# The first part of a down projection as 2x2 blocks with seven products, its sums made in the second block of the up projection

## The chip, the cores and the metric

The kernel runs on one core of one Trainium2 chip. The metric is device time in microseconds of one execution of the program; a profiled execution also gives the span from its first to its last instruction. TensorE (PE in the profile) multiplies, VectorE (DVE) and ScalarE (ACT) do the elementwise work, GpSimd (POOL) and SyncE (SP) issue DMAs here, as ACT does too.

## The reference

One layer of a streaming-encoder block, on x of 2048 tokens by 1024 channels in float32. The change touches only the last two lines' matrix products:

```python
h = rmsnorm(x, norm_mix_pre)
u_pool, u_glu, g_a, g_b = split(h @ w_in)
merged = sigmoid(g_a) * pool_mixer(u_pool, ...) + sigmoid(g_b) * conformer_conv(u_glu, ...)
x = x + rmsnorm(merged @ w_o, norm_mix_post)
h = rmsnorm(x, norm_mlp_pre)
f = square(relu(h @ w_up)) @ w_down        # (2048,1024)@(1024,4096), then (2048,4096)@(4096,1024)
return x + rmsnorm(f, norm_mlp_post)
```

## The kernel before

Activations lie transposed: channels on the 128 partitions, tokens along the free axis. A tile is 128x1024 float32 (512 KB): two chunks of 128 channels by a half block of 512 tokens (a "cell"), or an operand of weights. The 2048 tokens are two blocks b of 1024, each with two halves t.

**A product.** [...] `product` (L289) multiplies one weight tile (512 rows by 256 outputs) with two cells into one PSUM tile of 128x1024: two output chunks times four row chunks times three passes, 24 matmuls of 128x128x512, all issued in `matmuls` (L264, L268). Only this instruction form matters below. Every new weight tile costs one cast and one subtraction (`split_w`, L222, cast at L225), every new cell the same.

**Seven products for eight.** All large matrix products are done as 2x2 blocks with Winograd's seven products, numbered 1 to 7: 1 = A11 B11, 2 = A12 B21, and 5, 6, 3, 7, 4 use sums of blocks on one or both sides. `Octet` (L426) runs the seven for one octet of outputs, 512 rows by 512 columns of w_up with 1024 tokens, in three PSUM tiles (`ps_mm` has 3; x takes 1, 6, 7, 4, z takes 2, y takes 5, 3). `ORDER` is (1, 2, 6, 5, 7, 3, 4); the first two octets of a block are interleaved by `START`.

**up.** `mlp_up` (L1400) has eight octets u = 0 to 7 for each block. Output (m, t) of octet u, after ReLU and square, is stored to DRAM as `fd[b, u, (m, t)]`: m is the pair of chunks within the octet's two pairs, t the token half. `sink` also makes and stores the token sums that down needs ("t1", "t2", "t3", "t4"). Octets 0 and 1 of the second block load their weights' low parts and sums ("kept") rather than make them; the others load w_up and split it.

**down.** 4096 rows are four slabs s of 1024 (octets 2s and 2s+1 of up), 1024 outputs are two octets o. Inside each (s, o, b) stand again 2x2 blocks (outputs by pair of chunks m, rows by m, tokens by half t) with seven products i. A job (s, i, b) is two products, one for each o: `down_product` (L1737) accumulates over the four slabs in PSUM, so one i takes 4 slabs x 2 blocks x 2 octets = 16 products, and 7 x 16 = 112 products are all of down. `last_product` (L1751) takes each sum out into the outputs c00, c01, c11, u. i = 1, the block A11 B11 (rows and outputs of the first pairs, first token half), is "the first part": its result `c00[o, b]` is shared by all four outputs. Jobs run by i in `SHARED` (1, 5, 6, 3, 7), then `ALONE` (4, 2).

**Queues and order.** `load` issues on SP's queue, `store` on ACT's, `aside` on POOL's. Each queue and each engine works in the order a scheduler gives at build time; a DMA whose buffer isn't free holds all behind it on its queue. `lanes` hold background generators; `bg()` (L1475), called after every product, advances them one step. `then(f, octet, i)` (L1557) calls f after product i of an octet. `with behind()` (L170) orders instructions after the main line's last eviction. Pools: `p_big` 28 tiles (all taken by the split token sums of a block in up), `p_tr` 9, `p_fo` 5, weights raw `p_wr` 4, high and low parts 3 each.

**Around the change.** One job of down, `FILL`, is computed before up's second block (`filler`, L1957); its result goes to DRAM and is added in later. It is the first job, (0, 1, 0). In up's second block one lane runs `scales()`: `mlp_scale` (L1374) loads x1d, squares it into tiles of `p_fo` and sums it, for the last norm. During up's last octet the cells of down's first three jobs are loaded and split (L1986), so they lie ready when down begins; in the main loop of down the cells are fetched two jobs ahead and each new weight two at a time.

Of the kernel before, what the change touches and what calls it, by code (L numbers as in the profile page):

```python
# [62 lines left out]
def f32(ap):  # L63
    return ap.bitcast(F32)
# [3 lines left out]
def block_kernel(  # L68
# [616 lines left out]
    class Squares:  # L685
# [22 lines left out]
    p_big = pool("pbig", 28)  # L708
    p_tr = pool("ptr", 9)
    early = ExitStack()  # L710
    p_y = pool("py", 1, early)
    p_ss = pool("pss", 1, early)
    p_v = pool("pv", 2, early)
# [297 lines left out]
                load(zd[b, c - 1, 0], y[c - 1])  # L1011
            yield 1

    pw = [p_const.tile([P, CW], F32R, tag=f"pw{i}", name=f"pw{i}") for i in (0, 1)]

    def pool_weight():
        raw = mk(p_wr, "wr")[:, :CW]
# [356 lines left out]
    def mlp_scale(b, buf):  # L1374

        st = None
        for t in (0, 1):
            sq = Squares(buf)
            for c in range(0, CPS, 2):
                x = [mk(*buf) for _ in (0, 1)]  # L1380
                for i in (0, 1):
                    load(x[i], x1d[b, c + i, t])
                yield 1
                sq.add(x[0])
                sq.add(x[1])
            yield 1
            ss = sq.total()
            yield 1
            if st is None:
                st = root_psum()  # L1390
            root_acc(st, ss, inv_d, t * G)
        yield 1
        r = root_dve(st[:, : 2 * G])
        q = p_const.tile([P, 2 * G], F32, tag=f"q{b}", name=f"q{b}")
        mul(q, r, r)
        for t in (0, 1):
            q2[b, t] = q[:, t * G : (t + 1) * G]
        yield

    def mlp_up(b, parts):  # L1400
        def one(u):
            f = {}
            late = (b and u >= 2) or u >= 4

            def sink(m, t, ps, s):
                o = tr()
                if s is not None:
                    mark(add(o, ps, s))
                    ps = o
                mark(nc.scalar.activation(o, ps, AF.Relu))  # L1410
                nc.scalar.activation(o, o, AF.Square)
# [254 lines left out]

    def scales():
# [31 lines left out]
    def token_cells(s, i, b, home=TR, hi_home=BIG):  # L1699

        ready = s >= 2 or (b and s)
        a, m = {
            7: ("t3", None),
            1: ((0, 0), None),
            2: ((1, 0), None),
            6: ("t2", None) if ready else ("t3", (0, 0)),
            4: ("t4", None),
            5: ("t1", None) if ready else ((0, 1), (0, 0)),
            3: ((1, 1), None),
        }[i]  # L1710
        with tc.high_priority(offset=AHEAD):
            cells = []
            for j in (0, 1):
                u = 2 * s + j
                lo = mk(*home, F32R)
                t = f32(lo)
                load(t, fd[b, u, a])
                if m is not None:
                    t2 = mk(*home)
                    load(t2, fd[b, u, m])  # L1720
                    (add if i == 6 else sub)(t2, t, t2)
                    t = t2
# [7 lines left out]
                nc.scalar.copy(hi, t)  # L1730
                sub(lo, t, f32(hi))
                cells.append((hi, lo))
        return cells
# [1 line left out]
    acc = {}  # L1735

    def down_product(s, i, b, w, cells):  # L1737
        first = s == 0 or (s, i, b) == (1, 1, 0)
# [12 lines left out]
    def last_product(i, o, b, ps):  # L1751
# [9 lines left out]
            for h, p in spans(ps):  # L1761
                mark(add(c[:, h], of[:, h], p))

        if i == 1:
            if k in fill:
                c00[k] = mk(*BIG)
                load(c00[k], fill[k])
                to(c00[k], c00[k])
            else:
                taken(c00)  # L1770
        elif i == 5:
            taken(c11)
        elif i == 6:
            u[k], c01[k] = mk(*BIG), mk(*BIG)
# [182 lines left out]
    def filler():  # L1957
        s, i, b = FILL
        cells = fill.pop("cells")
        for o in (0, 1):  # L1960
# [6 lines left out]
            store(fill[o, b], t)  # L1967
            bg()

    cells = {}  # L1970
    merged = Parts(lambda ops: merged_parts(ops, cells))

# [8 lines left out]
    lanes += [Lane(1, chain)]  # L1981
    filler()
    octs = mlp_up(1, parts)
    then(lambda: lanes.extend([Lane(1, scales())]), octs[1])
    got = []
    for n, i in enumerate((5, 7, 3)):  # L1986
        then(lambda n=n: got.append(token_cells(*jobs[n], BIG, BIG if n == 2 else FO)), octs[-1], i)
    run(octs)
    empty()
    coming = got  # L1990
    for n, (s, i, b) in enumerate(jobs[:-SLABS]):
        if (s, i) == (0, ALONE[0]):
# [4 lines left out]
        if i in ALONE or b == 0 or (s, i) == FILL[:2]:  # L1997
            w = [weight_down(i, s, o) for o in (0, 1)]
        cells = coming.pop(0)
        while len(coming) < 2 and n + 1 + len(coming) < len(jobs):  # L2000
            job = jobs[n + 1 + len(coming)]
            coming.append(token_cells(*job, BIG if n < 4 else TR))
        down_product(s, i, b, w, cells)
    end = []
    for n, (s, i, b) in enumerate(END):
# [80 lines left out]
```

## Time and profile before

| what | value |
|---|---|
| median of 3 runs | 2181.39 us (2181.01 to 2182.33) |
| the profiled execution's own time | 2180.6 us |
| its span, first to last instruction | 2178.8 us |
| mean granted TensorE clock | 0.997 |
| matmuls recorded | 9678 |
| HBM traffic over the span | 253 GB/s |

The profiled execution is 0.8 us under the median of the runs, and 1.8 us of its own time lie outside the span. The page counts busy time of each engine; a matmul's 389 ns is its latency, and matmuls overlap, so the cost of one is read from the chain of waits (so many matmuls in so many us) and not from its mean. In the names, `up`, `down`, `wo` are PSUM tiles; `rb` is a small PSUM pool that some down sums use as well. Times in us are counted from the start of the span; up's second block begins near 1243, down's main part near 1556.4.

### The profile page before, as it was taken

The numbers are of one execution on the slowest core, as the hardware profiler recorded it, in microseconds if no ns is written. First come the engines' busy times: TensorE is split into PE (matmuls) and PEld (weight loads), VectorE is DVE, ScalarE is ACT, GpSimd is POOL, SyncE is SP. The second block draws the span as 40 slices with busy tenths as digits, with TensorE's granted clock in tenths as the row PEclk, the third lists the DMA queues.
The fourth block names the chain that finished last, engine by engine and source line by source line (L and its number), as shares of the span: only waits on it lengthen the run. The fifth ranks groups of instructions, "written<-read, shape, count | busy, mean of one in ns | idle before, by whom it ended". The sixth has DMA issues, their size and how long they took to land.

```text
span 2178.8 us, 25059 instructions
## 1 busy us (share of the span) xinstructions
PE 2159.4 (99%) x9678; PEld 1788.4 (82%) x9678; DVE 1614.7 (74%) x1593; ACT 1017.8 (47%) x1064; POOL 16.4 (1%) x39
## 2 busy tenths in 40 slices
PE   9999999999999999999999999999999999999998
PEld 7888888888888888888888878888888888888887
DVE  8997789998688998977757765756744746546786
ACT  6444454334543445555635775555622323334551
POOL 1000000000000000000000000000000000000000
PEclk9999999999999999999999999999999999999999
DMA  7688997778997788445787685644977875545882
GB/s 274 233 297 311 325 353 272 269 252 292 340 379 239 262 306 287 158 148 198 279 300 268 214 286 189 228 168 160 322 275 274 320 271 178 209 154 188 275 301 86
DMA packets 155625, 552.33 MB, mean 253 GB/s; under 512 B 17264, under 2 KB 19568, under 8 KB 155504
## 3 DMA queue, kind: packets, MB, share of 16 engines
q1 hardware_dynamic: 139696, 493.99, 63.7%
q10 hardware_dynamic: 12672, 46.14, 5.5%
q0 software_dynamic: 3136, 10.58, 1.3%
q8 instruction: 76, 1.25, 0.2%
q14 instruction: 45, 0.37, 0.1%
HBM read 366.00 MB, written 184.64 MB: 253 GB/s over the span
## 4 chain that ended last, share of the span: by engine, by line
PE 93%; DVE 3%; DMA 2%; issue 1%; ACT 1%; SPq 0%; DVEq 0%
PE up L268 26%; PE down L268 23%; PE wo L268 8%; PE ga L268 7%; PE gb L268 7%; PE glu L268 6%; PE rb L268 5%; PE B L268 4%; PE A L268 4%; PE pool L268 3%; DMA big<-xt 1%; PE rb L563 1%; DVE big L121 1%; PE mix L268 1%; DVE y L938 0%
## 5 line engine op out<-in xcount | busy, mean ns | idle before, releaser
L268 PE MATMUL up<-big,wh 128*128 128x512 f32 x1792 | 481.0, 390 | 2.2 <-DVE big L121 1.6
L268 PEld LDWEIGHTS up<-big,wh 128*128 128x128 f32 x1792 | 335.8, 188 | 74.0 <-DVE big L121 2.7
L225 ACT CAST wh<-wr 128x1024 fp32r<-128x1024 f32 x195 | 204.9, 1052 | 384.9 <-PE up L268 77.4
L938 DVE SCALAR_TENSOR_TENSOR y<-v,cst,y 128x1024 f32<-128x1024 f32 x240 | 307.2, 1280 | 2.8
L268 PE MATMUL up<-big,wl 128*128 128x512 f32 x896 | 276.1, 389 | 0.0
L268 PE MATMUL down<-big,wh 128*128 128x512 f32 x736 | 274.9, 389 | 0.0
L225 ACT CAST wh<-ws 128x1024 fp32r<-128x1024 f32 x126 | 132.4, 1052 | 252.8 <-PE up L268 63.6
L268 PE MATMUL down<-tr,wh 128*128 128x512 f32 x616 | 239.7, 389 | 0.0
L121 DVE TENSOR_TENSOR tr<-tr,big 128x1024 fp32r<-128x1024 f32 x100 | 120.5, 1222 | 117.3 <-ACT big L1730 116.8
L268 PE MATMUL down<-big,wl 128*128 128x512 f32 x664 | 204.5, 389 | 0.0
L121 DVE TENSOR_TENSOR wl<-ws,wh 128x1024 fp32r<-128x1024 f32 x118 | 143.9, 1220 | 75.5 <-ACT wh L225 75.3
L268 PEld LDWEIGHTS up<-big,wl 128*128 128x128 f32 x896 | 168.1, 188 | 34.8
L121 DVE TENSOR_TENSOR wl<-wr,wh 128x1024 fp32r<-128x1024 f32 x118 | 143.7, 1218 | 53.7 <-ACT wh L225 52.9
L1730 ACT CAST big<-tr 128x1024 fp32r<-128x1024 f32 x98 | 101.2, 1050 | 169.5 <-DMA tr<-fd 138.1
L268 PEld LDWEIGHTS down<-big,wh 128*128 128x128 f32 x736 | 138.2, 188 | 28.6
L268 PEld LDWEIGHTS down<-big,wl 128*128 128x128 f32 x664 | 124.6, 188 | 25.9
L268 PEld LDWEIGHTS down<-tr,wh 128*128 128x128 f32 x616 | 115.6, 188 | 24.0
L268 PE MATMUL wo<-big,wh 128*128 128x512 f32 x480 | 128.7, 390 | 0.0
L268 PE MATMUL glu<-big,wh 128*128 128x512 f32 x464 | 126.8, 394 | 1.2 <-DVE big L816 0.5
L268 PE MATMUL gb<-big,wh 128*128 128x512 f32 x448 | 120.0, 390 | 0.0
L268 PE MATMUL ga<-big,wh 128*128 128x512 f32 x448 | 120.0, 389 | 0.0
L268 PEld LDWEIGHTS wo<-big,wh 128*128 128x128 f32 x480 | 89.9, 188 | 18.5
(212 smaller groups left out, 3351.4 us busy)
## 6 DMA issues: line engine op xcount, KB each, us to landing
tr<-fd SPq DMA_DIRECT2D x110, 512.0 KB, 5.1
wr<-w_down SPq DMA_DIRECT2D x90, 512.0 KB, 5.8
wl<-kept SPq DMA_DIRECT2D x85, 512.0 KB, 4.6
kept<-wl SPq DMA_DIRECT2D x72, 512.0 KB, 6.1
wr<-w_up SPq DMA_DIRECT2D x64, 512.0 KB, 4.4
wr<-w_in SPq DMA_DIRECT2D x60, 512.0 KB, 5.3
fd<-tr ACTq DMA_DIRECT2D x54, 512.0 KB, 3.9
fd<-tr SPq DMA_DIRECT2D x46, 512.0 KB, 2.9
```

Source lines behind the costliest of these rows:

```text
L121: return nc.vector.tensor_tensor(o, a, b, op=ALU.subtract)
L225: nc.scalar.copy(hi[:, :n], src[:, :n])
L268: i = nc.tensor.matmul(ps, w[wp][:, (at + k) * P : (at + k + 1) * P], rhs[k][xp], start=start and n == 0, stop=stop and n == len(order) - ...
L563: nc.tensor.matmul(st[:, at + g : at + g + 1], ss[:, g * P : (g + 1) * P], inv_n, start=start is None or (start and g == 0), stop=stop, sk ...
L938: nc.vector.scalar_tensor_tensor(acc, v[:, k : k + TB], wk, acc, op0=ALU.mult, op1=ALU.add)
L1730: nc.scalar.copy(hi, t)
```

## The change

`SHARED` loses i = 1. The whole first part, the product of 2048 rows (the first pairs of all slabs) by 512 outputs with 1024 tokens, is itself cut into 2x2 blocks: outputs by octet o, rows by slab pairs (slabs n and n + 2 for n = 0, 1), tokens by block b. It is done with the seven products p of `LEVEL` = (1, 2, 6, 5, 7, 3, 4), each of two `product` calls (n = 0, 1), straight after up and before the jobs of down. The rest:

- the operand sums on the token side, T1 to T4, are made in up's second block: after product 1 of each octet (2 for octet 1) one tile (u < 4) or three (u >= 4) are loaded from DRAM into `fo` tiles, after its output (0, 0) they are subtracted in place, and stored by POOL's queue;
- the operand sums on the weight side (`level_weights`) are made in the same block, from its octet 1 on, ahead of `scales()`: 8 loads of w_down, 8 additions or subtractions, 8 stores by POOL's queue, in ten background steps;
- `mlp_scale` squares in place and waits longer between its steps; `p_fo` has 6 tiles, for which the pool weight's two tiles go into a pool that is closed by then; "t4" in `token_cells` is stored by POOL's queue;
- the filled job becomes (0, 7, 0), whose weight is a difference of two loaded tiles, and is added to `u` at job (1, 3, 0);
- during up's last octet the cells of p = 1 are loaded and split and those of p = 2 loaded, in place of the cells of three jobs.

In the built programs the change takes 48 matmuls off TensorE (two products of 24) and adds 47 instructions to VectorE, 19 casts and copies to ScalarE, 38 DMAs to SP's queue and 30 stores to POOL's. ScalarE keeps all its stores.

```diff
-        def add(self, src, scale=1.0):
-            sq = mk(*self.tmp)
+        def add(self, src, scale=1.0, own=False):
+            sq = src if own else mk(*self.tmp)
...
-                yield 1
-                sq.add(x[0])
-                sq.add(x[1])
+                yield 2
+                sq.add(x[0], own=True)
+                sq.add(x[1], own=True)
...
+            def fetch_other():
+                h = u - SLABS
+                for k, at in (
+                    (("T3", (1, h, (0, 0))), ("T2", (1, h, "T1")), ("T4", (0, u, (0, 0))))
+                    if u >= SLABS else (("T1", (0, u, (0, 0))),)
+                ):
+                    other[k] = fo()
+                    load(other[k], fd[at])
...
+                if b and (m, t) == (0, 0):
+                    for k, d in other.items():
+                        if k == "T4":
+                            sub(d, d, other["T2"])
+                        else:
+                            sub(d, o, d)
+                        keep(k, d, aside)
...
-            return Octet(w_up, u, b, parts, sink, "up", "sums" if u < 2 else None)
+            o = Octet(w_up, u, b, parts, sink, "up", "sums" if u < 2 else None)
+            return then(fetch_other, o, 2 if u == 1 else 1) if b else o
...
-    p_fo = pool("pfo", 5)
+    p_fo = pool("pfo", 6)
...
-    SHARED, ALONE = (1, 5, 6, 3, 7), (4, 2)
+    SHARED, ALONE = (5, 6, 3, 7), (4, 2)
...
-                        load(fd[b, u, "t4"], t4)
+                        aside(fd[b, u, "t4"], t4)
...
-    FILL = jobs.pop(0)
...
+    FILL = (0, SHARED[-1], 0)
+    jobs.remove(FILL)
...
+    LEVEL = ORDER
+    def level_weights():
+        for n in (0, 1):
...
+            a21, a22 = get(n, 1), get(n + 2, 1)
+            yield 1
+            a11 = get(n, 0)
+            add(a22, a21, a22)
+            kept_as(5, a22)
+            yield 1
+            sub(a21, a11, a21)
+            kept_as(7, a21)
+            yield
+            sub(a11, a22, a11)
+            kept_as(6, a11)
+            a12 = get(n + 2, 0)
+            yield 1
+            sub(a12, a12, a11)
+            kept_as(3, a12)
+            yield
...
+    def level_product(p, w, cells):
+        a = {1: "x", 2: "z", 6: "x", 7: "x", 4: "x", 5: "y", 3: "y"}[p]
+        if p in (1, 2, 5):
+            sums_of[a] = psum("down")
+        ps = sums_of[a]
+        for n in (0, 1):
+            product(ps, w[n], cells[2 * n : 2 * n + 2], ...)
+            if n == 0:
+                bg()
+        with tc.high_priority(offset=AHEAD):
+            if p in (1, 5, 6, 4):
+                o = taken_of[p] = mk(*BIG)
+                mark(nc.scalar.copy(o, ps))
+                if p == 4:
+                    c00[1, 0] = o
+            else:
+                of, k = {2: (1, (0, 0)), 7: (5, (1, 1)), 3: (6, (0, 1))}[p]
+                c00[k] = taken_of[of]
+                mark(add(c00[k], ps, c00[k]))
+        bg()
...
-    then(lambda: lanes.extend([Lane(1, scales())]), octs[1])
+    then(lambda: lanes.extend([Lane(1, chain_of(level_weights(), scales()))]), octs[1], 1)
     got = []
-    for n, i in enumerate((5, 7, 3)):
-        then(lambda n=n: got.append(token_cells(*jobs[n], BIG, BIG if n == 2 else FO)), octs[-1], i)
+    then(lambda: got.append(level_loads(LEVEL[0], BIG)), octs[-1], 5)
+    then(lambda: got.append(level_loads(LEVEL[1], BIG)), octs[-1], 3)
+    then(lambda: got.append(level_parts(got.pop(0), 40)), octs[-1], 7)
     run(octs)
     empty()
     coming = got
+    w = [level_weight(LEVEL[0], k) for k in (0, 1)]
+    here, coming = coming[0], coming[1:]
+    for n, p in enumerate(LEVEL):
+        with behind():
+            if n + 1 < len(LEVEL):
+                following = [level_weight(LEVEL[n + 1], k) for k in (0, 1)]
+                there = level_parts(coming.pop(0))
+            else:
+                following = [weight_down(jobs[0][1], jobs[0][0], o) for o in (0, 1)]
+            if n + 2 < len(LEVEL):
+                coming.append(level_loads(LEVEL[n + 2], (BIG, TR, BIG, TR, BIG)[n]))
+            else:
+                coming.append(token_cells(*jobs[n + 2 - len(LEVEL)], BIG))
+        level_product(p, w, here)
+        w, here = following, there
```

`level_weight` loads a tile of w_down (p = 1, 2, 4) or a stored sum (5, 6, 7, 3) and splits it; `level_loads` loads the four cells of a product, `level_parts` splits them.

More of the change, by code (lines that the diff above doesn't have):

```diff
@@ L710, in block_kernel @@
     early = ExitStack()
+    p_pw = pool("ppw", 1, early)
     p_y = pool("py", 1, early)
@@ L1737, in down_product @@
     def down_product(s, i, b, w, cells):
-        first = s == 0 or (s, i, b) == (1, 1, 0)
+        first = s == 0 or (s, i, b) == (1, *FILL[1:])
         for o in (0, 1):
@@ L1762, in to @@
                 mark(add(c[:, h], of[:, h], p))
[L1764 to L1771, printed above, removed]
+        if i == 5:
             taken(c11)
@@ L1968, in filler, with get, kept_as @@
             bg()
+    LEVEL = ORDER
+    level = {}
+    def level_weights():
+        for n in (0, 1):
+            def get(s, o):
+                t = fo()
+                load(t, w_down[2 * s + o, 0])
+                return t
+            def kept_as(k, t):
+                level[k, n] = dram("level")
+                aside(level[k, n], t)
+            a21, a22 = get(n, 1), get(n + 2, 1)
[14 more added lines that the diff above has]
+            yield
@@ new lines, in level_weight, with level_loads @@
+    def level_weight(p, n):
+        with tc.high_priority(offset=AHEAD):
+            t = mk(p_wr, "wr")
+            o = {1: 2 * n, 2: 2 * (n + 2), 4: 2 * (n + 2) + 1}.get(p)
+            load(t, level[p, n] if o is None else w_down[o, 0])
+            return split_w(t)
+    def level_loads(p, home):
+        b, at, k = {
+            1: (0, 0, (0, 0)), 2: (0, SLABS, (0, 0)), 3: (1, SLABS, (0, 0)),
+            5: (1, 0, "T1"), 6: (1, SLABS, "T2"), 7: (1, SLABS, "T3"), 4: (1, SLABS, "T4"),
+        }[p]
+        with tc.high_priority(offset=AHEAD):
+            los = [mk(*home, F32R) for _ in range(SLABS)]
+            for u, lo in enumerate(los):
+                load(f32(lo), fd[b, u + at, k])
+        return los
@@ new lines, in level_parts @@
+    def level_parts(los, sooner=AHEAD):
+        with tc.high_priority(offset=sooner):
+            return [parted(mk(*BIG, F32R), lo) for lo in los]
+    sums_of, taken_of = {}, {}
+    def level_product(p, w, cells):
[4 more added lines that the diff above has]
+        for n in (0, 1):
+            product(
+                ps, w[n], cells[2 * n : 2 * n + 2],
+                start=p in (1, 2, 5) and n == 0, stop=p in (2, 4, 3) and n == 1,
+            )
+            if n == 0:
+                bg()
+        with tc.high_priority(offset=AHEAD):
+            if p in (1, 5, 6, 4):
[8 more added lines that the diff above has]
+        bg()
@@ L2001, in block_kernel @@
             job = jobs[n + 1 + len(coming)]
-            coming.append(token_cells(*job, BIG if n < 4 else TR))
+            with behind() if n < 8 else nullcontext():
+                coming.append(token_cells(*job, BIG if n < 4 else TR))
         down_product(s, i, b, w, cells)
```

13 lines of the change are left out of this document (9 added, 4 removed).

## The prediction

> **What bounds the kernel now.** I read the page's busy times first, then the list of TensorE's waits from up's second block to the end, then the chain of waits where down begins.
>
> ```profile
> span 2178.8 us, 25059 instructions
> PE 2159.4 (99%) x9678; PEld 1788.4 (82%) x9678; DVE 1614.7 (74%) x1593; ACT 1017.8 (47%) x1064; POOL 16.4 (1%) x39
> ```
>
> TensorE is busy 99% of the span, VectorE 74%, ScalarE 47%. The next list covers 1240 to 2178 us (engine, line, what it waited for: total us, times, longest), and the chain is cut to the first products of down.
>
> ```profile
> PE up L268 <- DVE big L121: 1.6, 2, 0.8
> PE down L268 <- DVE big L118: 0.8, 1, 0.8
> PE rb L654 <- DVE sp L634: 0.5, 1, 0.5
> PE up L268 <- ACT big L218: 0.2, 1, 0.2
> ...
> 1556.79 5.44 PE down L268 x24
> 1562.23 5.44 PE rb L268 x24
> 1567.67 16.32 PE down L268 x72
> ```
>
> In 938 us TensorE waited 3.1 us. A product is 24 matmuls in 5.44 us, 226.7 ns each (16.32 / 72). So the time is the number of products, plus whatever a change makes TensorE wait. The stretches that the change touches, as busy us of each engine, granted clock, DMA share and GB/s:
>
> ```profile
> 1243.10:1276.00 32.90, 31.13 (x143) 24.96 (x141) 28.50 (x35) 27.77 (x34) 0.00 (x0) 1.00 0.95 328
> 1270.00:1324.00 54.00, 53.03 (x232) 43.07 (x231) 28.59 (x25) 33.84 (x35) 0.00 (x0) 1.00 0.62 220
> 1276.00:1400.00 124.00, 124.00 (x555) 102.63 (x554) 72.32 (x72) 72.36 (x73) 0.00 (x0) 1.00 0.61 215
> 1400.00:1518.00 118.00, 118.00 (x530) 97.80 (x529) 73.85 (x73) 62.28 (x62) 0.00 (x0) 1.00 0.46 165
> 1518.00:1556.40 38.40, 38.40 (x171) 31.78 (x170) 30.04 (x26) 28.50 (x29) 0.00 (x0) 1.00 0.93 330
> 1556.40:1632.60 76.20, 76.20 (x338) 63.10 (x337) 37.21 (x32) 20.21 (x21) 0.00 (x0) 1.00 0.78 286
> ```
>
> The reader is to see three tight places: the entry of up's second block (VectorE 28.5 of 32.9, DMA share 0.95), its last octet (0.93), and between them room: VectorE 146.2 of 242 us, DMA 0.46 to 0.61.
>
> **The products removed.** The first part is 4 slabs x 2 blocks x 2 octets = 16 products before. After it is seven products of two calls, 14. The filled job stays at two products, only of another i. So 2 x 24 = 48 matmuls go, 48 x 226.7 ns = 10.88 us, all of it on the path, since TensorE has no other wait there. This is the whole gain; nothing else is removed that TensorE waits for, as its 3.1 us of waits stand at places that the change leaves.
>
> [...]
>
> **Sums made in up's second block.** By the order of the built programs, VectorE gets 16 subtractions for T1 to T4 and 8 for the weights. Prices of one operation and one transfer:
>
> ```profile
> L121 DVE TENSOR_TENSOR wl<-wr,wh 128x1024 fp32r<-128x1024 f32 x118 | 143.7, 1218 | 53.7 <-ACT wh L225 52.9
> L225 ACT CAST wh<-wr 128x1024 fp32r<-128x1024 f32 x195 | 204.9, 1052 | 384.9 <-PE up L268 77.4
> L1730 ACT CAST big<-tr 128x1024 fp32r<-128x1024 f32 x98 | 101.2, 1050 | 169.5 <-DMA tr<-fd 138.1
> wr<-w_down SPq DMA_DIRECT2D x90, 512.0 KB, 5.8
> x1d<-big POOLq DMA_DIRECT2D x8, 512.0 KB, 5.4
> ```
>
> 24 x 1.22 = 29.3 us on VectorE, which is busy 204.7 of 313.3 us there (28.5 + 72.3 + 73.9 + 30.0): 75% after. It lies beside TensorE's products; if that cover were gone it would cost all 29.3. Squaring in place adds nothing, and `scales()` only moves later into the slack after 1324.
>
> At the entry there is no slack, and two T1 subtractions fall there:
>
> ```profile
> 1262.13 2.35 DVE L121 TENSOR_TENSOR tr<-big,big 128x1024 f32<-128x1024 f32 x2
> 1264.70 1.05 ACT L218 CAST big<-tr 128x1024 fp32r<-128x1024 f32 x1
> 1270.47 2.35 DVE L121 TENSOR_TENSOR tr<-big,tr 128x1024 f32<-128x1024 f32 x2
> 1271.84 1.06 ACT L1411 ACTIVATE tr<-tr 128x1024 f32<-128x1024 f32 x1
> 1273.87 2.36 DVE L121 TENSOR_TENSOR big<-tr,big 128x1024 fp32r<-128x1024 f32 x2 [1.05 <-ACT big L218]
> 1275.15 1.64 PE L268 MATMUL up<-big,wh 128*128 128x512 f32 x5 [0.75 <-DVE big L121]
> ```
>
> In the build's order octet 0's T1 stands just ahead of the pair at 1262.13. The pair's first result, now at 1263.3, comes at 1264.5, and the cast that wants it starts at 1264.70 anyway: nothing. Octet 1's T1 stands between the pairs at 1270.47 and 1273.87. It needs the square that ends at 1272.9, runs to 1274.1, and so moves the second pair, and the product that waits for it at 1275.15, by 0.25 us. Taken: +0.25 (0 to 1.2, one operation). The filled job's two more weight loads and subtractions stand some 30 us ahead of their product, beside the products of wo: nothing, and 2 x 1.22 if VectorE were full there.
>
> **DMAs of the sums.** The weight sums take ten steps, one a product, from 1270 to 1324: 8 loads, 8 stores, and 2 stores of T1, 18 x 0.524 MB = 9.4 MB in 54 us, 175 GB/s on top of the row's 220: 395 GB/s. What the DMA engines give when they are full, and what it cost TensorE then:
>
> ```profile
> DMA packets 2834, 10.30 MB, mean 382 GB/s; under 512 B 323, under 2 KB 323, under 8 KB 2832
> PE gb L268 <- DMA wl<-kept: 1.3, 1, 1.3
> wl<-kept SPq DMA_DIRECT2D x7, 512.0 KB, 4.3
> ```
>
> The first row is of 535 to 562 us, the second the one wait of TensorE for a DMA in the whole span, which lies there, the third of 1270 to 1324. 395 is 13 over 382, a backlog of 0.7 MB or 1.8 us by the end of the stretch. In the way stand the low parts of the weights (wl<-kept), issued behind the new loads on SP's in-order queue, with two products (10.88 us) until they are used, and landing in 4.3. Bounds: 0 (the entry ran at 0.95 with the same loads and no such wait) and 2.6 (1.3 us for each 27 us). I take 0.6, near the lower end, since the reader and its ring of three buffers are those of the entry.
>
> [...]
>
> Later octets add six transfers in 38 us, 83 GB/s on 165 to 215: room. A T load that comes late holds VectorE's queue, with the next low halves behind it:
>
> ```profile
> 1520.30 1.22 DVE L121 TENSOR_TENSOR wl<-ws,wh 128x1024 fp32r<-128x1024 f32 x1
> ```
>
> That one is for the last octet's third product, due at 1556.4 - 5 x 5.44 = 1529.2: 7.7 us early. Nothing, below a lateness of 7.7.
>
> **The seven products themselves.** A step (one p, 10.88 us) needs 6 loads (4 cells, 2 weights), 3.15 MB, 289 GB/s, under the 382 above; on ScalarE 6 casts (6.3) and an eviction, on VectorE 6 subtractions (7.3) and at times an addition. The eviction is this row's kind:
>
> ```profile
> 1241.45 1.00 ACT L1965 COPY tr<-down 128x1024 f32<-128x1024 f32 x1
> 1563.52 1.02 ACT L1410 ACTIVATE tr<-up 128x1024 f32<-128x1024 f32 x1
> ```
>
> In a line: eviction 1.0, four casts 4.2, two weight casts 2.1, the last subtraction 1.2 = 8.5 of 10.88, 2.4 us to spare. Loads are asked for a step or two earlier. The accumulators are evicted while the next p runs on another, so a wait there has 10.88 us of cover. Cost taken 0, bounds 0 and the first rival's price.
>
> **Sum.** -10.88 + 0.25 + 0.6 = -10.0 on the profiled execution's 2180.6: 2170.6. The runs' median lies 0.8 above it: 2171.4. Its own range: 2169.8 (no added cost, and the runs' 0.7 of spread) to 2174.
>
> **Rivals.** *The section starves (slower).* If a step's loads land only after it has begun, the line is 8.5 + 5.8 = 14.3 us, 3.4 over, and six steps lose 20.6: 2192. It decides from a landing 2.4 us into a step; from 4.1 (10.0 / 6 more) the gain is gone. For it: four stores of up's last sums stand in SP's queue among these loads and hold them until VectorE has made those sums, and less is split beforehand (one p, not three jobs). Against: the same engines moved 286 GB/s in this stretch with a share of 0.78. 0.13.
>
> *A hitch at p = 2 only.* Its cells' casts stand behind the last ReLU of up on ScalarE. That ran at 1563.52, 7.1 us after its product. If it stays there: 1564.5 + 4.2 + 1.05 = 1569.8, where the product is due at 1567.3: 2.5, hence 2173.9. Against: it was held by other jobs' casts that waited for loads, which are gone. 0.10.
>
> *The weight sums crowd the kept parts.* Each of the seven wl<-kept of that stretch makes TensorE wait 1.3: 9.1 in place of 0.6, 2179.9, no change. It decides from a landing of 10.9 us instead of 4.3. For it the 395 against 382, against it the entry. 0.11.
>
> That fewer products are run than said is certain from the build; no chance goes there.
>
> **How the numbers follow.** Likeliest 0.66, hitch 0.10, crowding 0.11, starving 0.13. What this kernel's measurement can tell is about 0.2%, 4.4 us on 2181.39: faster below 2177.0, which the first two are (0.76); same 0.11; slower 0.13. The range must reach into the crowding case, as the first two hold only 0.76: 2169.8 to 2179.
>
> **What would show it.** Matmuls 9630 on the page. TensorE's waits from 1240 on still under 5 us, none on a DMA; from up's last product to the first of job (0, 5, 0) 76.2 us (14 products); wl<-kept landing in 5 to 8 us between 1270 and 1324. A row of TensorE waiting for casts or subtractions of the level's cells over 5 us would make the prediction wrong, as would one for wl<-kept.

## The result, and the profile after

The changed kernel takes 2169.64 us (median of 6 runs, 2165.67 to 2171.63), the kernel before 2181.55 us beside it: ratio 0.9952, 95% interval 0.9941 to 0.9962; by the ratio that is 10.5 us less, while the two medians lie 11.9 apart. Run again in two later series it gave 2170.68 us (ratio 0.9957, 0.9943 to 0.9972) and 2170.91 us (0.9955, 0.9943 to 0.9968). Forecast were 2171.4 us, 1.8 us over the first median, and a range whose lower end, 2169.8, lies 0.16 us above it; the two later medians lie inside the range.

The page of the changed kernel, the two rows that answer to those of before:

```profile
span 2167.4 us, 25192 instructions
PE 2146.1 (99%) x9630; PEld 1778.2 (82%) x9630; DVE 1666.4 (77%) x1640; ACT 1036.4 (48%) x1083; POOL 32.3 (1%) x69
```

48 matmuls fewer, VectorE at 77% instead of 74%. TensorE's waits from 1240 us to the end, changed kernel:

```profile
PE up L268 <- DVE big L121: 1.8, 2, 1.0
PE down L268 <- DVE big L118: 0.8, 1, 0.8
PE rb L654 <- DVE sp L634: 0.6, 1, 0.6
PE up L268 <- ACT big L218: 0.2, 1, 0.2
```

They are the places of before: 3.4 us instead of 3.1, none for a DMA and none in the new section. The chain of waits of the changed kernel, cut to the filled job, the first products of down and the last matmuls, and the last matmuls of the kernel before:

```profile
1231.68 10.88 PE down L268 x48
...
1556.14 92.48 PE down L268 x408
...
2152.31 1.73 PE rb L574 x7
```

```profile
2163.83 1.73 PE rb L574 x7
```

The second row is seventeen products without a gap (408 matmuls in 92.48 us, 226.7 ns each): the fourteen of the new section and the first three of job i = 5. From down's first matmul to the last group it is 596.17 us, before 2163.83 - 1556.79 = 607.04: 10.87 us less. The busy times by stretch, columns as in the prediction:

```profile
1270.00:1324.00 54.00, 52.82 (x231) 42.93 (x230) 35.06 (x31) 32.72 (x33) 4.06 (x8) 1.00 0.94 364
1276.00:1400.00 124.00, 124.00 (x553) 102.80 (x552) 78.79 (x69) 70.43 (x71) 5.32 (x10) 1.00 0.79 298
1518.00:1556.40 38.40, 38.40 (x170) 31.76 (x170) 30.31 (x35) 22.78 (x24) 1.60 (x3) 1.00 0.72 276
1556.40:1632.60 76.20, 76.20 (x338) 63.08 (x337) 56.81 (x51) 44.44 (x46) 0.00 (x0) 1.00 0.85 332
```

The weight sums took the DMA share between 1270 and 1324 from 0.62 to 0.94 and the rate from 220 to 364 GB/s; the section of seven products moves 332 GB/s with VectorE at 75%.

Two numbers sort all the profiles below: how long up's second block takes (first matmul of it to down's first) and how long the rest (to the last group, L574). What lies ahead of up's second block isn't in them. In us, from the timeline and the chain of each:

| kernel | up's second block | from down on |
|---|---|---|
| before | 313.52 | 607.04 |
| the change, three profiles | 313.74, 317.21, 314.36 | 596.17, 596.17, 596.17 |
| fill_alone | 313.47 | 607.03 |
| sums_unused | 321.89 | 607.04 |
| sums_light | 313.58 | 607.04 |
| two_more | 314.61 | 607.59 |
| one_ahead | 313.97 | 601.49 |
| copies | 331.43 | 596.16 |
| late_parts | 313.59 | 601.10 |
| t4_later | 313.62 | 596.21 |
| late_copies | 316.49 | 596.17 |
| sp_stores | 313.61 | 596.15 |

### The profile page after: what moved, and what is told of

Same layout as the page of the kernel before. It is cut to its first block, busy times and chain, and to the rows that moved or that the text cites. A ratio compares the mean times of both kernels' runs of the same rounds, so it can differ in the third digit from the quotient of the medians.

```text
span 2167.4 us, 25192 instructions
## 1 busy us (share of the span) xinstructions
PE 2146.1 (99%) x9630; PEld 1778.2 (82%) x9630; DVE 1666.4 (77%) x1640; ACT 1036.4 (48%) x1083; POOL 32.3 (1%) x69
## 4 chain that ended last, share of the span: by engine, by line
PE 92%; DVE 3%; DMA 2%; ACT 1%; issue 1%; SPq 0%; DVEq 0%; ACTq 0%
PE up L268 28%; PE down L268 24%; PE wo L268 7%; PE ga L268 7%; PE glu L268 5%; PE gb L268 5%; PE B L268 4%; PE rb L268 4%; PE A L268 4%; PE pool L268 3%; DVE big L121 1%; DMA tr<-yd 1%; DMA wl<-kept 1%; PE rb L563 1%; PE mix L268 1%
## 5 line engine op out<-in xcount | busy, mean ns | idle before, releaser
L268 PE MATMUL up<-big,wh 128*128 128x512 f32 x1792 | 480.9, 390 | 2.1 <-DVE big L121 1.8
L268 PEld LDWEIGHTS up<-big,wh 128*128 128x128 f32 x1792 | 335.9, 188 | 73.8 <-DVE big L121 2.9
L268 PE MATMUL down<-big,wh 128*128 128x512 f32 x856 | 296.4, 390 | 0.0
L268 PE MATMUL up<-big,wl 128*128 128x512 f32 x896 | 276.2, 389 | 0.0
L268 PE MATMUL down<-big,wl 128*128 128x512 f32 x704 | 216.9, 389 | 0.0
L268 PE MATMUL down<-tr,wh 128*128 128x512 f32 x552 | 214.9, 389 | 0.0
L268 PEld LDWEIGHTS up<-big,wl 128*128 128x128 f32 x896 | 168.2, 188 | 34.8
L268 PEld LDWEIGHTS down<-big,wh 128*128 128x128 f32 x856 | 160.7, 188 | 33.4
L121 DVE TENSOR_TENSOR wl<-wr,wh 128x1024 fp32r<-128x1024 f32 x122 | 148.7, 1220 | 45.8 <-ACT wh L225 44.7
L121 DVE TENSOR_TENSOR tr<-tr,big 128x1024 fp32r<-128x1024 f32 x92 | 110.5, 1222 | 73.8 <-ACT big L1748 64.2
L268 PEld LDWEIGHTS down<-big,wl 128*128 128x128 f32 x704 | 132.2, 188 | 27.4
L1748 ACT CAST big<-tr 128x1024 fp32r<-128x1024 f32 x82 | 84.4, 1050 | 112.2 <-DMA tr<-fd 96.2
L121 DVE TENSOR_TENSOR big<-big,big 128x1024 fp32r<-128x1024 f32 (+1 forms) x90 | 108.0, 1221 | 30.3 <-ACT big L1748 11.8
L268 PE MATMUL wo<-big,wh 128*128 128x512 f32 x480 | 128.6, 390 | 0.4 <-ACT tr L1312 0.4
L268 PE MATMUL glu<-big,wh 128*128 128x512 f32 x464 | 125.2, 391 | 1.3 <-ACT wh L225 0.9
L268 PEld LDWEIGHTS down<-tr,wh 128*128 128x128 f32 x552 | 103.6, 188 | 21.4
L268 PE MATMUL gb<-big,wh 128*128 128x512 f32 x448 | 120.0, 390 | 0.0
L268 PE MATMUL ga<-big,wh 128*128 128x512 f32 x448 | 119.9, 389 | 0.0
```

What stands on the lines that cost most here:

```text
L121: return nc.vector.tensor_tensor(o, a, b, op=ALU.subtract)
L268: i = nc.tensor.matmul(ps, w[wp][:, (at + k) * P : (at + k + 1) * P], rhs[k][xp], start=start and n == 0, stop=stop and n == len(order) - ...
```

## The experiments

**fill_alone: only the filled job is another.** Against the kernel before:

```diff
-    FILL = jobs.pop(0)
...
+    FILL = (0, SHARED[-1], 0)
+    jobs.remove(FILL)
...
-        first = s == 0 or (s, i, b) == (1, 1, 0)
+        first = s == 0 or (s, i, b) == (1, *FILL[1:])
...
+        if (s, i, b) == (1, 3, 0):
+            for o in (0, 1):
+                t = fo()
+                load(t, fill[o, 0])
+                add(u[o, 0], u[o, 0], t)
```

> The kernel before with one part of the change alone: the job that fills wo is (0, 7, 0) in place of (0, 1, 0), so that its result is added to u instead of c00. 9678 matmuls as before. Theory (the gain is two products of 5.44 us, nothing else): no change, 2181 to 2182 us, ratio 0.9995 to 1.0005. Rival (part of the 11.9 us that the medians show comes from the other job in the gap, as the 1.0 us over 10.88 would have it): 2180.5 or less. Rival (its two more weight loads and subtractions delay wo): 2183 to 2184.

Measured: 2179.75 us (12 runs, 2176.43 to 2184.82), ratio 0.9992 (0.9982 to 1.0002). That is 1.7 us less with 2.2 either side; the median lies in the first rival's range, and by itself it decides nothing. But both stretches of the table are those of before within 0.05 us, and so is the one that holds the filled job, from the first product of wo to the first of up's second block: 1243.05 - 1154.13 = 88.92 us, before 1243.27 - 1154.36 = 88.91. The fill brings nothing.

**two_more: two products given back among the seven.**

```diff
+        if p in (2, 3):
+            extra = psum("down")
+            product(extra, w[1], cells[2:4], start=True, stop=True)
+            nc.scalar.copy(tr(), extra)
```

> The changed kernel with two products of 24 matmuls more among the seven (at p = 2 and p = 3, on cells and weights that are there, into an accumulator that only a copy reads; no loads, two evictions of 1.0 us on ScalarE). 9678 matmuls. Theory (TensorE is the bound throughout the section): 2169.6 + 10.88 = 2180.5 us, all of the change's gain given back. Rival (TensorE has idle time among the seven that the products fill, or the gain lies elsewhere): 2175 or less.

Measured: 2180.42 us (12 runs), ratio 1.0002 (0.9994 to 1.0011). The gain is gone: 607.59 us from down on, 11.42 over 596.17, of which 10.88 are the two products and 0.3 a wait at the section's exit; 0.2 stay open. TensorE is the bound through the section.

**sums_unused: the sums without the seven products.** Against the changed kernel; the section of `level_product` is left out:

```diff
-    SHARED, ALONE = (5, 6, 3, 7), (4, 2)
+    SHARED, ALONE = (1, 5, 6, 3, 7), (4, 2)
...
-    then(lambda: got.append(level_loads(LEVEL[0], BIG)), octs[-1], 5)
-    then(lambda: got.append(level_loads(LEVEL[1], BIG)), octs[-1], 3)
-    then(lambda: got.append(level_parts(got.pop(0), 40)), octs[-1], 7)
+    for n, i in enumerate((5, 7, 3)):
+        then(lambda n=n: got.append(token_cells(*jobs[n], BIG, BIG)), octs[-1], i)
```

> The changed kernel without its seven products: T1 to T4 and the weight sums are made and stored in up's second block as in the change, and used by nothing; down's first part runs as sixteen plain products. 9678 matmuls. Theory (all added work of up's second block is covered but for some 0.2 us at its entry): 2181.4 + 0.2 to 0.9 = 2181.6 to 2182.3 us, up's second block 0.2 us longer than before. Rival (the sums cost more and the products bring more than 10.88): 2183 or more. Rival (the weight sums crowd the kept parts): 2190.

Measured: 2187.65 us (6 runs, 2185.54 to 2188.64), ratio 1.0031 (1.0019 to 1.0043): 6.7 us slower than before, where 0.2 to 0.9 were expected. The timeline of its last octet in up (start, duration, instruction, and in brackets what it waited for):

```profile
1552.82 1.04 ACT L1748 CAST big<-big 128x1024 fp32r<-128x1024 f32 x1 [5.58 <-DMA big<-fd]
...
1553.90 1.22 DVE L121 TENSOR_TENSOR big<-big,big 128x1024 fp32r<-128x1024 f32 x1 [5.39 <-ACT big L1748]
1555.04 1.22 DVE L118 TENSOR_TENSOR tr<-up,tr 128x1024 f32<-128x1024 f32 x1
...
1556.40 2.90 PE L268 MATMUL up<-big,wh 128*128 128x512 f32 x6 [4.33 <-DVE tr L118]
```

A prefetched cell landed late; ScalarE stood at its cast, VectorE behind it at its low part (the operand minus its cast, the high part; a product adds up high x high, high x low and low x high), and the eviction that TensorE needed was queued behind that. The kernel before fetches three jobs at the same places and has no such wait; here the loads and stores of the sums stand beside them. And the wait is not all of the price. The stretch of the wait and the one after it:

```profile
1552.07:1556.40 4.33, 0.00 (x0) 0.03 (x1) 2.50 (x3) 2.10 (x3) 0.00 (x0) 0.93 0.86 351
1556.40:1562.00 5.60, 5.60 (x13) 4.43 (x14) 3.58 (x4) 4.09 (x5) 0.00 (x0) 0.50 0.59 159
```

For 5.6 us TensorE ran at a granted clock of 0.50, 13 matmuls where 25 fit; the product took 8.60 us in place of 5.44. The wait of 4.3 us cost 7.5.

**sums_light: the same sums, the prefetch as the change does it.** Two jobs instead of three, loads first, casts and subtractions later:

```diff
+    then(lambda: got.append(raw(*jobs[0])), octs[-1], 5)
+    then(lambda: got.append(raw(*jobs[1])), octs[-1], 3)
+    then(lambda: got.append(paired(got.pop(0), 40)), octs[-1], 7)
```

> As sums_unused (T1 to T4 and the weight sums made and stored, used by nothing; down's first part as sixteen plain products, 9678 matmuls), but the cells of the first two plain jobs are prefetched in up's last octet as the change does it: loads first, casts and subtractions three products later, not load, cast and subtraction at once for three jobs. Theory (the 6.7 us of sums_unused came from ScalarE and VectorE held by late cells in the last octet, and from the clock of 0.5 that followed TensorE's wait of 4.3 us; the sums themselves are covered): ratio 1.0000 to 1.0005, no wait of TensorE over 1.0 us in up's second block. Rival (the sums themselves cost it, DMAs or VectorE full): 1.002 or more, again a wait of some us in the last octet.

Measured: 2180.99 us (11 runs), ratio 1.0000 (0.9991 to 1.0010); no wait in up's second block over 1.0 us. So the 24 sums and their 48 transfers cost nothing that these runs can tell (2 us either side), and what sums_unused lost came from the sums together with the way the next cells were fetched. Whether fewer jobs or the later casts made the difference wasn't tried.

**one_ahead: loads one step ahead, not two.**

```diff
-                there = level_parts(coming.pop(0))
-            if n + 2 < len(LEVEL):
-                coming.append(level_loads(LEVEL[n + 2], (BIG, TR, BIG, TR, BIG)[n]))
-            else:
+                there = level_parts(level_loads(LEVEL[n + 1], (BIG, TR)[n % 2]))
+            if n + 2 >= len(LEVEL):
```

> The changed kernel with the four cells of each p loaded at the beginning of the step before (with the two weights), not a step earlier: nothing of them lies in up but p = 1. 9630 matmuls. The prediction's rival (a step's loads land 5.8 us into the step that must also cast and subtract them: 5.8 + 8.5 = 14.3 us a step in place of 10.88): 3.4 us for each of six steps, 2169.6 + 20.6 = 2190 us. Theory of cover (only the first pair of cells is due at the step's end, the second 5.44 us later; six loads of 0.524 MB at 380 GB/s take 8.3 us, and the first pair with its casts and subtractions another 2.3 us or so: 10.6 of 10.88): 0 to 0.5 us a step, 2170 to 2173 us.

Measured: 2175.08 us (12 runs, 2171.2 to 2178.66), ratio 0.9974 (0.9964 to 0.9984), some 4.8 us over the change. Not one step of the seven waits, though their loads fill the DMA engines. The windows of the section, and of the exit from it, with the matmuls that waited there:

```profile
1574.00:1590.00 16.00, 16.00 (x72) 13.28 (x71) 12.92 (x11) 10.92 (x12) 0.00 (x0) 1.00 1.03 411
1590.00:1606.00 16.00, 16.00 (x72) 13.24 (x72) 8.60 (x8) 8.68 (x10) 0.00 (x0) 1.00 1.03 412
...
1657.80:1661.00 3.20, 3.20 (x8) 2.52 (x9) 3.20 (x3) 1.04 (x1) 0.00 (x0) 0.50 1.01 342
```

```profile
1656.47 0.50 PE L268 MATMUL down<-big,wh 128*128 128x512 f32 x1 [1.56 <-ACT big L1748]
1657.80 0.80 PE L268 MATMUL down<-big,wh 128*128 128x512 f32 x1 [0.83 <-DVE big L121]
```

The debt is paid at the first jobs of i = 5, whose loads stand behind the section's. From down on it takes 601.49 - 596.17 = 5.3 us more: 2.4 of waits, and most of the rest the clock of 0.50 behind them. The rival's 3.4 us a step is not there; the theory of cover held in the section and missed its exit.

**late_parts: p = 1 split behind up's last ReLU.**

```diff
-    then(lambda: got.append(level_parts(got.pop(0), 40)), octs[-1], 7)
...
-    here, coming = coming[0], coming[1:]
+    with behind():
+        here = level_parts(coming.pop(0))
```

> The changed kernel with the casts and subtractions of p = 1's four cells behind up's last ReLU (as the prediction's rival had it for p = 2), not in up's last octet; the loads stay. The prediction's way of pricing a hitch (the wait alone: the first cast at 1557.2 where the product is due at 1556.1, then one pair after the other): about 2 us for the first cell and 1 to 3 for the next ones, 2172 to 2174.5 us. Rival (after a wait of over 1.5 us the granted clock is 0.5 for 3 to 6 us, as in sums_unused and one_ahead): 1.7 to 3.2 us more, 2174 to 2178 us, with a clock of 0.5 in the rows after 1558.

Measured: 2173.57 us (12 runs, 2171.99 to 2179.36), ratio 0.9974 (0.9964 to 0.9983). The two matmuls that waited, and the stretch behind them:

```profile
1557.28 0.49 PE L268 MATMUL down<-big,wh 128*128 128x512 f32 x1 [2.05 <-ACT big L1074]
1558.54 2.27 PE L268 MATMUL down<-big,wh 128*128 128x512 f32 x5 [0.77 <-DVE big L121]
```

```profile
1558.54:1562.00 3.46, 3.46 (x9) 2.72 (x10) 3.46 (x4) 3.46 (x5) 0.00 (x0) 0.54 0.90 302
```

2.8 us of waits; from down's due start the rest took 601.10 instead of 596.17, 4.9 more, so 2.1 are the clock's. The median, 2173.57, lies in the range of the pricing by the wait alone, 2172 to 2174.5, and just below the rival's 2174 to 2178; so the runs don't decide for the rival. The profile shows what it said: waits as priced, and on top of them 2.1 us lost at a clock of 0.54.

**copies: 8.4 MB more beside the weight sums.**

```diff
                 load(t, w_down[2 * s + o, 0])
+                aside(dram("spare"), w_down[2 * s + o, 0])
+                aside(dram("spare"), w_down[2 * s + o, 0])
```

> The changed kernel with 16 more transfers of 0.524 MB between buffers in DRAM, two beside each load of a weight sum, issued by GpSimd (nothing else uses them): 8.4 MB more in some 54 us, 19.6 + 8.4 = 28 MB where 412 GB/s carry 22.2. Theory (a crowded stretch costs nothing until the low parts of the weights land later than the two products, 10.9 us, that they are asked for ahead; they landed in 7.3): the backlog of 5.8 MB is 14 us, landings pass 10.9 and TensorE waits for wl from kept, 3 to 12 us in all, and as much again where the granted clock halves after a wait: 2173 to 2190 us. Rival (the low parts keep their share against the other queue and land in under 10.9 us): no wait, 2170 us.

Measured: 2186.28 us (7 runs), ratio 1.0030 (1.0019 to 1.0041). DMA issues from 1270 to 1324 (transfers, KB each, median us from issue to landing), first in the changed kernel, then with the copies:

```profile
fo<-w_down SPq DMA_DIRECT2D x8, 512.0 KB, 8.6
wl<-kept SPq DMA_DIRECT2D x7, 512.0 KB, 7.3
```

```profile
wl<-kept SPq DMA_DIRECT2D x7, 512.0 KB, 11.5
fo<-w_down SPq DMA_DIRECT2D x6, 512.0 KB, 17.1
```

With them the matmuls that waited:

```profile
1291.41 0.80 PE L268 MATMUL up<-big,wh 128*128 128x512 f32 x1 [5.72 <-DVE big L121]
1328.50 1.65 PE L268 MATMUL up<-big,wl 128*128 128x512 f32 x3 [6.68 <-DMA wl<-kept]
```

The low parts land in 11.5 us, over the 10.88 they are asked for ahead, and TensorE waits for them, once. The other wait had not been foreseen: the addition of a weight sum stood on VectorE for its load, which landed after 16.9 us, with the next operand's low part behind it. In the change the same loads land in 7.3 and 8.6: no wait, but no longer far from one.

**change_again and change_third: the change itself, unaltered.**

> The changed kernel once more, unaltered, on the chip of the next three runs. Theory: ratio 0.9950 (10.88 us off 2181, with at most 0.3 us of added cost), from the start of down's first product to the last matmuls 596.2 us as in the first profile. What differs between profiles of one kernel should lie in the granted clock of the first 100 us (0.98 in the profile of before, 1.00 in that of the change, about 1.7 us). Rival (the 11.9 us between the medians are a gain of their own, over 10.88): 0.9945 or less.

> The changed kernel unaltered, beside t4_later on the same chip: ratio 0.9950 to 0.9957; in the profile a wait of 0 to 1.8 us for an eviction near 1475, and from down's start to the last matmuls 596.2 us.

Their times stand above; both profiles take 596.17 us from down on. But up's second block took 317.21 us in the one and 314.36 in the other: the profiles differ in more than the first 100 us, where the expectation had looked for it. VectorE's timeline in change_again shows where:

```profile
1465.00 1.23 DVE L121 TENSOR_TENSOR fo<-fo,fo 128x1024 f32<-128x1024 f32 x1 [4.08 <-DMA fd<-fo]
1466.14 1.22 DVE L121 TENSOR_TENSOR wl<-wr,wh 128x1024 fp32r<-128x1024 f32 x1
1472.94 1.23 DVE L118 TENSOR_TENSOR ws<-wr,wr 128x1024 f32<-128x1024 f32 x1 [5.58 <-DMA wr<-w_up]
1474.08 1.22 DVE L118 TENSOR_TENSOR tr<-up,tr 128x1024 f32<-128x1024 f32 x1
...
1475.35 1.80 PE L268 MATMUL up<-big,wh 128*128 128x512 f32 x6 [1.81 <-DVE tr L118]
```

The first row is T4 of octet u = 5. VectorE stands 4.1 us at it (the bracket names a store that landed at about the same time; T4's own load, asked for at 1455.1, landed 9.7 us later, at 1464.8); the low part behind it frees its `wr` buffer late, so the next load of w_up is asked for late, so the weight's sum is late, and with it the eviction queued behind. This chain is not all: counted from the start of the block, the load is asked for 0.8 us later than in the first profile, and it then takes 5.5 us instead of 4.4 to land; why isn't shown. TensorE waits 1.8 us, and the clock drops behind it:

```profile
1475.35:1479.50 4.15, 4.15 (x12) 3.26 (x13) 3.83 (x4) 3.67 (x4) 0.00 (x0) 0.67 0.28 116
```

The product is due at 1475.35 - 1.81 = 1473.54, 230.9 us after the first matmul of up's second block (1242.61). In the first profile of the change that is 1473.3, and the same eviction ended there at 1473.24: no wait, with 0.1 us to spare. In change_third it came 0.6 late; in the profile of before it ended at 1472.34, some 1.6 us ahead of its product. The other eight profiles with T4 at this place have waits of 0 (sums_light, late_parts and sp_stores), 0.2, 0.6, 0.7, 0.9 and 1.2 us here; the expectation of t4_later, below, leaves out the zeros of sums_light and late_parts.

**t4_later: T4's subtraction behind the next eviction.**

```diff
-                        if k == "T4":
-                            sub(d, d, other["T2"])
-                        else:
+                        if k != "T4":
                             sub(d, o, d)
-                        keep(k, d, aside)
+                            keep(k, d, aside)
+                elif "T4" in other:
+                    d = other.pop("T4")
+                    with behind():
+                        sub(d, d, other["T2"])
+                        keep("T4", d, aside)
```

> The changed kernel with T4's subtraction put on VectorE behind the next eviction of its octet, not ahead of the weights' low parts. In the change its load lands 8.8 to 9.9 us after it is asked for, VectorE stands 2.9 to 4.1 us for it near 1460, the buffer of the weight behind it comes free later, so does the next load of w_up, and with it the eviction that a product near 1475 waits for: 0, 0.2, 0.9, 1.8, 0.6 and 0.7 us in six profiles that hold these sums. Theory (that chain is the cause): no wait of TensorE for an eviction (L118) between 1440 and 1500, no wait of VectorE for a T load ahead of it; the mean falls by 0.5 to 2 us against the change, 2167.5 to 2170, ratio 0.9940 to 0.9952. Rival (the load of w_up itself is late, whatever VectorE does): the wait of 0 to 1.8 us stays.

Measured: 2170.6 us (5 runs, 2169.08 to 2174.83), ratio 0.9961 (0.9949 to 0.9974), beside 2170.91 of the change in the same series: no difference that can be told. The timeline of VectorE, at the same place:

```profile
1467.64 1.22 DVE L121 TENSOR_TENSOR wl<-wr,wh 128x1024 fp32r<-128x1024 f32 x1 [1.85 <-ACT wh L225]
1473.11 1.23 DVE L118 TENSOR_TENSOR ws<-wr,wr 128x1024 f32<-128x1024 f32 x1 [4.25 <-DMA wr<-w_up]
1474.25 1.22 DVE L118 TENSOR_TENSOR tr<-up,tr 128x1024 f32<-128x1024 f32 x1
1475.39 1.22 DVE L121 TENSOR_TENSOR fo<-fo,fo 128x1024 f32<-128x1024 f32 x1
```

This profile runs some 5 us later (its opening is longer; the first matmul of up's second block is at 1247.51), so the eviction ends at 1475.5 where its product is due at 1478.4: 2.9 us of slack. VectorE no longer waits for T4 ahead of the low part. That TensorE doesn't wait shows little by itself, since it doesn't in sums_light, late_parts and sp_stores either; but there, with T4 in its old place, the slack is 1.0, 0.6 and 0.9 us. So T4's place costs some 2 us of slack, by one profile. That moving it lowers the mean of many runs is likely and isn't shown.

**late_copies: two transfers beside the T loads of the last four octets.**

```diff
+                for _ in range(2 if u >= SLABS else 0):
+                    aside(dram("spare"), w_down[0, 0])
```

> The changed kernel with two transfers of 0.524 MB between buffers in DRAM beside the T loads of each of the last four octets of up (nothing uses them): T4 lands some 2.6 us later (1.05 MB at 400 GB/s). Theory (the place near 1475 has 2 us of slack without T4 and none with it): waits of 1 to 3 us there and perhaps in the octets beside it, with the clock at 0.5 after each over 1.5 us: 2172 to 2180 us. Rival (the prediction's own slack of 7.7 us holds for every octet): no wait, 2169 to 2171 us.

Measured: 2184.22 us (9 runs), ratio 1.0019 (1.0009 to 1.0029). It does not test what it was made for. The transfers wait for nothing, and the scheduler put all eight at the kernel's start; the first 100 us have TensorE busy for 84.8 us (96.0 in the change) at a clock of 0.91, and up's second block begins 12.3 us later. So the price is the opening's. The wait behind T4 is there as well, 1.2 us, within the 0 to 1.8 of the unaltered change; the granted clock is 0.65 in the 3.27 us behind it, and up's second block is 2.75 us longer than in the first profile of the change.

**sp_stores: the sums stored by SP's queue.**

```diff
-                        keep(k, d, aside)
+                        keep(k, d)
...
-                aside(level[k, n], t)
+                load(level[k, n], t)
```

> The changed kernel with the stores of T1 to T4 and of the weight sums in SP's queue, where the loads are, in place of GpSimd's. Each waits there for VectorE's sum, with the loads of up's next weights behind it. Theory (the loads are asked for two products, 10.9 us, ahead, and a sum is late by 3 to 4 us at most): 0 to 2 us, most of it near 1475: 2170 to 2173 us. Rival (the queue that the change chose for them is what keeps the loads on time): 5 us or more, 2175 us or more, TensorE waiting in most octets.

Measured: 2168.8 us (4 runs, 2166.53 to 2173.05), ratio 0.9950 (0.9936 to 0.9964), and no wait in up's second block beside the entry's; that is below the theory's 2170 to 2173. Which queue stores the sums makes no difference that these four runs can tell (3 us either side).

## Why the prediction was right, and where it was off

- *Bound and products removed* (-10.88): right. From down on it is 10.87 us less in each of three profiles, and two_more gives it back.
- *Sums on VectorE under cover* (0): right as a whole, by sums_light; the one place where it isn't is the step below (*Later octets*).
- *Entry* (+0.25): right. The wait that was 0.75 at 1275.15 is 0.97 in the changed kernel, +0.22:

```profile
1274.45 1.64 PE L268 MATMUL up<-big,wh 128*128 128x512 f32 x5 [0.97 <-DVE big L121]
```

- *DMAs of the weight sums* (+0.6, 0 to 2.6): too high, it cost 0. The landing of 7.3 us lies in the 5 to 8 that were named, and two products of cover held. The rival of crowding had its point of decision, 10.9, about right: copies passes it and waits. The stretch moved 364 GB/s at a DMA share of 0.94, under the 382 against which the backlog was worked out; and 382 is not the most that these engines gave, since one_ahead's section moved 412 for 16 us at a share of 1.03.
- *Later octets* ("nothing, below a lateness of 7.7"): this is the step that failed. The 7.7 us were the slack of one low part in the last octet, taken for all. In octet u = 5 the same kind of wait delays a buffer, a load and a sum ahead of an eviction, and the slack there, 1.6 us before, is 0.1 us in the first profile of the change. TensorE waits 0, 1.8 and 0.6 us there in the three profiles of the change, which with the clock behind it cost 0, 3.5 and 0.6. For up's second block +0.85 was forecast; the three profiles have +0.22, +3.69 and +0.84, a mean of 1.6, nearly all of it at a place that was priced at nothing. That the sum came out close all the same is luck in part: 0.6 too much for the DMAs stands against a mean of 1.4 too little here.
- *The seven products* (0): right, no wait. one_ahead shows why the starving rival's line of 14.3 us was no bound: it asked that all of a step's work be done before the step begins, while the second pair of cells is only due 5.44 us into it.
- *Hitch at p = 2*: it did not come, as its "against" had it. Its casts do stand behind the last ReLU of up (L1420), but nothing holds that any more: it runs at 1556.18, at once behind its product and not 7.1 us later. ScalarE, changed kernel:

```profile
1556.18 1.03 ACT L1420 ACTIVATE tr<-up 128x1024 f32<-128x1024 f32 x1 [2.03 <-PE up L268]
1557.10 3.89 ACT L1074 CAST big<-big 128x1024 fp32r<-128x1024 f32 x4
...
1563.44 1.05 ACT L1421 ACTIVATE tr<-tr 128x1024 f32<-128x1024 f32 x1
```

- *The rivals' prices* counted the wait alone. late_parts, sums_unused and change_again show 1.7 to 3.2 us more for each, from the clock; had a rival come true, its time could have been too low by as much at each wait. The profile of before had shown it at 762 us, where a wait of 1.87 is followed by this row:

```profile
765.00:769.00 4.00, 4.00 (x15) 3.19 (x14) 1.95 (x5) 1.47 (x2) 0.53 (x1) 0.73 0.52 154
```

- *The range*: its lower end allowed 0.7 us for the runs, read off three runs 1.3 us apart. Thirty runs of the kernel before in one later series lie between 2176.32 and 2187.76. Of the 11.5 us by which the last groups of the two profiles lie apart, 1.7 are from the first 94 us, ahead of anything that the change touches (half of it is lost again by the start of up's second block): noise of an execution, not gain. About 0.4 of what is lost again is a place that no term counted: in wo, near 1186, TensorE waits 0.4, 0 and 0.2 us for a copy (L1312) in the three profiles of the change, 1.2 in two_more and in sp_stores, and not at all in before and fill_alone. Its cause wasn't followed.

## What to carry to other kernels

Here, with TensorE busy for 99% of the span, work taken from it was worth its own time (10.87 us for products of 10.88), and added work under cover was free only where each in-order queue that it joined had slack at that place (no added wait in sums_light; 4.33 us in sums_unused, 1.81 in change_again): take the slack from the nearest eviction or buffer behind the new wait in every stage, not from one stage. Split a prefetch into loads now and casts later; a cast that stood on its load held two engines in sums_unused, ScalarE for 5.58 us and VectorE for 5.39. Price a wait of TensorE at its own length where the clock holds and at 1.7 to 1.9 times that where it falls behind the wait (4.33 us cost 7.5, 2.8 cost 4.9, 1.81 cost 3.5); the length alone doesn't tell which.

## What the runs showed of the hardware

Behind some waits of TensorE the granted clock was as low as 0.50, and behind others of nearly the same length, at the same place, it stayed at 1.00. Waits of 4.33 us, 2.05 + 0.77, 1.87, 1.81 and 1.56 + 0.83 have behind them, in the rows shown above, a mean clock of 0.50 over 5.60 us, 0.54 over 3.46, 0.73 over 4.00, 0.67 over 4.15 and 0.50 over 3.20. But near 760 us, in code that the change leaves as it is, TensorE waits for the same instruction in all fourteen profiles: 1.87 us in that of before, with the clock of 0.73 shown above behind it, and 1.84 in t4_later, with 1.00:

```profile
762.02 1.02 PE L563 MATMUL rb<-inv_d,tr 128*128 128x1 f32 x8 [1.87 <-DVE tr L118]
```

```profile
767.43 1.02 PE L563 MATMUL rb<-inv_d,tr 128*128 128x1 f32 x8 [1.84 <-DVE tr L118]
770.40:774.40 4.00, 4.00 (x19) 3.30 (x19) 3.56 (x7) 3.03 (x4) 0.53 (x1) 1.00 0.42 110
```

In nine of the fourteen the clock fell there, behind waits of 1.17 to 1.99 us, and in five it held, behind 1.29 to 1.84. The wait near 28.3 us of the opening, with narrow matmuls behind it, is as mixed: 0.92 us in sp_stores and 1.33 in change_third, and the stretch behind it in this order:

```profile
30.00:36.00 6.00, 6.00 (x22) 4.80 (x22) 5.94 (x9) 2.19 (x3) 0.52 (x1) 0.72 0.78 261
```

```profile
30.00:36.00 6.00, 6.00 (x28) 4.94 (x27) 5.83 (x13) 2.99 (x3) 0.00 (x0) 1.00 0.74 262
```

Six matmuls fewer in six microseconds, behind the shorter wait. Among the wide matmuls alone (L268) single waits of 0.61 us in sums_unused (near 1474.6) and of 0.97, 1.12 and 1.16 in the changed kernel (at 1274.45, 389.90 and 558.61) left the clock at 1.00, 1.18 us in late_copies lowered it (to 0.65 in the 3.27 us behind it), and 1.25 us near 560 in the profile of before and 1.45 near 573 in late_copies left it. So executions of the same code differ by this too, and what decides between two waits of one length is not shown here.
